# Hymba-style block with 32 routed experts: groups of three experts between the pairs, a weight ring of 22 places instead of 20, and packed small parameters

## The chip, the cores and the metric

The kernel runs on one core of a Trainium2 chip. The metric is the time of one execution on the device in microseconds, as the median of several runs. A profiled execution gives the trace that all rows below come from. In the rows PE is the matrix engine, PEld its weight loads, DVE the vector engine, ACT the scalar engine, POOL GpSimd, and SP the engine whose queue issues nearly all transfers (SPq).

## The reference, cut to what matters

One layer over 512 tokens of width 1024, all in float32. Attention comes first, the mixture of experts second.

```python
h = rms_norm(x, g_attn); proj = h @ w_in                  # 1024 -> 3072 columns
o_da = diff_attention(q1, q2, k1, k2, v, rel_bias, lam)   # 4 heads, two softmax maps each
o_sb = stick_breaking(q, k, v)                            # 8 heads
x = x + concat(rms_norm(o_da), rms_norm(o_sb)) @ w_o
h2 = rms_norm(x, g_ffn)
gsel = argmax(h2 @ wg + bg)                               # 1 of 4 expert groups
e1, e2 = top_k((h2 @ we + be)[gsel], 2)                   # 2 of its 8 experts
# for each token: the gated sum over its two experts e of
y = (silu(h2 @ w1[e]) * (h2 @ w3[e])) @ w2[e]             # 1024 -> 512 -> 1024
x = x + gate * y
```

There are 32 experts, each with three matrices of 2 MiB: 192 MiB of weights. All of them are read once in every execution, whatever the routing says.

## The kernel before, in words

**Weights as tiles of 1 MiB.** Each expert has six tiles of 128 partitions by 2048 floats: two halves of w1, two of w3, two of w2. `load_parts` issues them on SP's queue, one transfer each (L714), in the order in which the products use them. A tile lives in a place of a ring (`ring_tile`, list `slots`). The places are buffers that attention used earlier: `bt`, `qs`, `kl`, `kh` (the q8 pool), `e0`, `e1`, `n0`, `n1`, the split projection weights `w_h`, `w_l`, and the attention outputs `ma`, `mb`. The two `ma` places are used once only, because the output sums (`sums`) move into that buffer. A transfer into a place waits on SP until the last product that reads the tile there before is done, and every transfer behind it on SP waits too. One more tile, the second half of w2 of expert 1, goes to the buffers `yh` and `yl` (`load_last`, L723).

**Places of experts.** The first `FIXED` experts keep their number as their place, so their weights can be loaded before the router has run. The others are sorted by how many tokens they got, most first; `sort_experts` and `name_experts` (L1094, the int32 row `who_i`) tell SP which expert stands at a place, and SP reads that into a register (L697) before it can issue the loads. Places 0 to 19 hold up to 64 tokens (`SLOTS`), places 20 to 31 (`SMALL`) up to 32.

**Groups.** PE works through 13 groups in the order of the list `groups`: two experts of 64 token columns each, or four of 32. Either way the 128 columns of a group are one pass of the matrix engine: products whose columns lie apart run side by side. A group has 16 steps in `hidden` (w1 in two halves, w3 in two halves, four steps each; products at L1222) and 8 in `outputs` (w2; L1278). Between the steps PE gathers the tokens of the next group (L1164, L926) and adds the outputs of the one before (`combine`, L1325 and L1326). Group 7 (`PAUSE`) also holds the branch to code for experts with more tokens than slots (L1342).

**The opening.** The transposed input and the projection weights `w_raw` (pieces of 256 KiB in 4 buffers) are loaded by turns. ACT and DVE split each into a rounded high part and a rest (`x_high`, `x_low`, `high`, `low`), and PE multiplies the parts at L313. Until then `keep_clock(20)` keeps PE busy with 20 products that nothing reads (L220, two records each). ACT also squares the four tiles of `x` for the norm (`square`, L243).

**The tail.** In the last group w3's second half and w2 are loaded in smaller cuts, expert after expert for each cut, and the output is computed in five column pieces (`TAIL`, `last_product`, `last_sum`).

Of the kernel before, what the change touches and what calls it, by code (L numbers as in the profile page):

```python
# [30 lines left out]
FIXED = 4  # L31
# [63 lines left out]
def tile_block(ctx: ExitStack, tc: tile.TileContext, a: dict, out: bass.AP):  # L95
# [45 lines left out]
    oh_rel, vneg = r_tile[0:32, 0, 0:640], r_tile[0:4, 1, 0:640]  # L141
    lamv, lam_p = r_tile[:, 0, 640:896].rearrange("p (a b) -> p a b", a=4), r_tile[:, 0, 896:960]
    rb = r_tile[0:32, 1, 640:644]
# [44 lines left out]
    g_col = const.tile([P, KC], F32, name="g_col")  # L188
    nc.scalar.dma_start(g_col, a["g_attn"][0].rearrange("(p k) -> p k", k=KC))
# [3 lines left out]
    for k in range(2, KC, 2):  # L193
        load_xT(k, k + 2)
        load_w()
    for t in range(NT):
        nc.sync.dma_start(x_t[t], x_in[t])
    gqk = const.tile([P, 2], F32, name="gqk")
    gsub = const.tile([P, 1], F32, name="gsub")
    gsb = const.tile([P, 1], F32, name="gsb")  # L200
    col = lambda ap, n: bass.AP(tensor=ap.tensor, offset=ap.offset, ap=[[1, n], [1, 1]])
    for m in range(2):
        rows = slice(64 * m, 64 * m + 64)
        nc.sync.dma_start(gqk[rows, 0:1], col(a["qn_g"], 64))
        nc.sync.dma_start(gqk[rows, 1:2], col(a["kn_g"], 64))
# [9 lines left out]

    def keep_clock(n, tag="mm"):

        pb = bank(tag, (P, P))
        for _ in range(n):
            nc.tensor.matmul(pb, lhsT=ones_f, rhs=ones_f, start=True, stop=True)  # L220

    keep_clock(20)
# [29 lines left out]
    for n in range(KC // 2):  # L252
        x_high(2 * n)
        high[n]()
        x_low(2 * n)
        low[n]()
        x_high(2 * n + 1)
        x_low(2 * n + 1)

    bt = pool_q8.tile([P, 4, 512], F32, tag="bt", name="bt")  # L260
    vdram = dram.tile([4, 640], F32, name="vdram")
    def small_loads():
        nc.sync.dma_start(rb, a["rel_bias"])
        nc.sync.dma_start(oh_rel, a["rel_onehot"])
        for m in range(2):
            nc.sync.dma_start(gsb[64 * m:64 * m + 64], col(a["sb_out_g"], 64))
        nc.sync.dma_start(gsub, col(a["subln_g"], 128))
        for i, n in enumerate(("lam_q1", "lam_k1", "lam_q2", "lam_k2")):
            s = a[n]
            nc.sync.dma_start(lamv[:, i], bass.AP(tensor=s.tensor, offset=s.offset, ap=[[0, P], [1, 64]]))  # L270
# [103 lines left out]
    def h_rows(i):  # L374


        pbs = [bank("mm", (P, 2, 256)) for _ in range(2 if i == 0 else 0)]
        for k in range(0, KC // 2, 2):
            for t0, pb in zip((0, 2), pbs):
                yield from rows_bundles(h_high, h_low, split[i], t0, pb, range(k, k + 2), k == 0, False)  # L380
        for t0 in (0, 2):
            pb = pbs[t0 // 2] if pbs else bank("sc" if (i, t0) == (1, 0) else "mm", (P, 2, 256))
            yield from rows_bundles(h_high, h_low, split[i], t0, pb, range(KC // 2 if pbs else 0, KC), not pbs)
            yield t0, pb
# [261 lines left out]
    for i, (g, n, j) in enumerate(ORDER):  # L646
# [10 lines left out]
    groups = [(0, 2), (2, 2), (20, 4), (4, 2), (6, 2), (8, 2), (10, 2), (24, 4), (12, 2), (14, 2), (16, 2), (18, 2),  # L657
              (28, 4)]
# [3 lines left out]
    slots = [("q8", tag, 2) for tag in ("bt", "qs", "kl", "kh")] + [("xs", "e0", 1), ("xs", "e1", 1)]  # L662
    slots += [("q8", tag, 2) for tag in ("qs", "kl", "kh")] + [("n", "n0", 1), ("n", "n1", 1)]
    slots += [("mx", "ma", 1), ("mx", "ma", 1), ("mx", "mb", 2)]
    slots += [("w8", tag, 2) for tag in ("w_h", "w_l", "w_h", "w_l")]
    slots += [("mx", "mb", 2)]
    slots[0] = ("q8", "bt", 1)

    def ring_tile():

        pool, tag, bufs = slots[ring[0] % len(slots)]
        ring[0] += 1
        if tag == "ma":
            if ring[0] > len(slots):
                return ring_tile()
# [15 lines left out]
    def load_parts(i):  # L691
        last = i == NG - 1
        first, n_exp = groups[i]
        if first < FIXED:
            who = [first + e for e in range(n_exp)]
        else:
            who = [nc.values_load(place_id[0][0:1, first + e:first + e + 1], engines=[mybir.EngineType.SP],  # L697
                                  min_val=0, max_val=NE - 1) for e in range(n_exp)]
        t = {}
        for n, h in hidden_order(i) + [("w2", 0), ("w2", 1)]:  # L700
            src = {"w1": w1, "w3": w3, "w2": w2}[n]
# [3 lines left out]
            for c, m in zip(cuts, cuts[1:]):  # L705
                for e in range(n_exp):
                    if (i, n, h, e) == (0, "w2", 1, 1):
                        continue
                    if c == 0:
                        t[n, h, e] = ring_tile()  # L710
                    dst, part = t[n, h, e], expert(who[e], h)(src)
                    if first >= FIXED:
                        part = part.rearrange("o p f -> p (o f)")
                    nc.sync.dma_start(dst[:, c:m], part[:, c:m])  # L714
                    if m == 2048:
                        yield t
# [9 lines left out]
    loads, ahead = load_parts(0), load_parts(1)  # L726

# [29 lines left out]
    gfp = const.tile([P, 2, 4], F32, name="gfp")  # L757
# [7 lines left out]
    def router_loads():  # L765
        nc.sync.dma_start(gfp, a["g_ffn"])
        raw_r = pool_at.tile([P, KC, 64], F32, tag="qn", name="raw_r", bufs=2)
        parts = {"w_router_g": raw_r[:, 0:1, 0:32], "w_router_e": raw_r[:, 1:5]}
        for n, r in (("w_router_g", 4), ("w_router_e", 32)):
            parts[n] = parts[n].rearrange("p a b -> p (a b)").rearrange("p (h c) -> p h c", h=2)  # L770
            nc.sync.dma_start(parts[n], a[n].rearrange("p h r c -> p h (r c)"))
        for src, c0, n in ((a["b_router_g"], 0, 4), (a["b_router_e"], 4, 32)):
            nc.sync.dma_start(rbias[:, c0:c0 + n], bass.AP(tensor=src.tensor, offset=src.offset, ap=[[0, P], [1, n]]))
# [14 lines left out]
        def gains():  # L788
            for n, c0, w in (("w_router_g", 0, 4), ("w_router_e", 4, 32)):
                nc.vector.tensor_tensor(wr[:, :, c0:c0 + w], parts[n].rearrange("p h (r c) -> p (h r) c", r=4),  # L790
                                        gfp.rearrange("p h r -> p (h r)").unsqueeze(2).to_broadcast([P, KC, w]),
                                        op=ALU.mult)
# [121 lines left out]
    def match(oh, rk, ts_):  # L914
        n = ts_.stop - ts_.start
        m, w = oh.shape[2:]
# [3 lines left out]
    def gather_part(px, oh, h, ts_):  # L920

        for t in ts_:
            x2 = x_tile[0][:, t, h * 512:(h + 1) * 512].rearrange("p (r b) -> p r b", r=4)
            one = oh[:, t].rearrange("p e s -> p (e s)").bitcast(F32)
# [38 lines left out]
    for t in range(NT):  # L963
        square(t)
    token_scales()
    wv.fill(16)
# [23 lines left out]
    next(ahead)  # L990
# [21 lines left out]
    oh0 = pools["n"].tile([P, NT, 2, SLOTS], F32R, tag="oh", name="oh", bufs=1)  # L1012
    def half_match(n, t):
# [3 lines left out]
        match(oh0, rank[:, :, 0:2], slice(t, t + 2))  # L1017
# [32 lines left out]
    for _ in range(7):  # L1050
        next(ahead)
# [72 lines left out]
    def one_hot(rk, second=False):  # L1124
        n = rk.shape[-1]
        shape = [P, NT, n, P // n]
        if second:
            oh = wk("oht", shape, F32R, bufs=2)
        else:
            oh = pools["n"].tile(shape, F32R, tag="oh", name="oh", bufs=1)  # L1130
        match(oh, rk, slice(0, NT))
        return oh

    def dispatch(oh, p, px=None):
# [3 lines left out]
        ohs = [oh[:, t].rearrange("p e s -> p (e s)") for t in range(NT)]  # L1138
        n_exp, w_exp = oh.shape[2:]
        rows = [slice(w_exp * e, w_exp * e + w_exp) for e in range(n_exp)]  # L1140
        d = {"px": px, "parts": rows}

        spare = not isinstance(p, int)
# [43 lines left out]
        def finish(tag="mm"):  # L1187
# [15 lines left out]
            m = 3 * n_exp  # L1203
            g4 = pools["n"].tile([P, NT, 12], F32, tag="g4" + own, name="g4", bufs=bufs)
            c = 0 if spare else 6 * p
            for u, pb in enumerate(pbs):
                nc.scalar.copy(oht[:, 2 * u:2 * u + 2], pb[:, :, 0])
                nc.vector.tensor_copy(g4[:, 2 * u:2 * u + 2, :m], pb[:, :, 1, c:c + m])
            for e, part in enumerate(rows):
                x = 6 * (e // 2) + 2 * (e % 2)  # L1210
# [9 lines left out]
    def hidden_product(ph, d, n, h, r, e, w):  # L1220
        part = d["parts"][e]
# [3 lines left out]
    def hidden(p, t, d, between):  # L1225
# [3 lines left out]
        for n, h in hidden_order(p):  # L1229
            if n not in ph:  # L1230
                ph[n] = bank("mm")
            for r in range(4):
                for e in range(len(d["parts"])):
                    hidden_product(ph, d, n, h, r, e, t[n, h, e][:, r * HID:(r + 1) * HID])
# [53 lines left out]
    def outputs(t, ht, d, between):  # L1288
# [3 lines left out]
        for c in range(2):  # L1292
            py.append(bank("sc"))
            for j in range(4):
                for e, part in enumerate(d["parts"]):
# [33 lines left out]
    def overflow():  # L1329
# [12 lines left out]
        with tc.If(rounds > 0):  # L1342
            move(rank_s[:, :, SMALL:], SLOTS // 2)
            with tc.For_i(0, rounds, 1):
                move(rank_s, -SLOTS)
                with tc.For_i(0, NP, 1) as iv:
# [5 lines left out]
                    dd = dispatch(one_hot(rk), own)  # L1352
# [5 lines left out]
                    for n, h in hidden_order(1):  # L1358
                        for e in range(2):
                            src = (w1 if n == "w1" else w3)[bass.ds(who[e], 1), h].rearrange("o p f -> p (o f)")  # L1360
                            for r in range(0, 4, 2):
                                w = half_slot(src[:, r * HID:(r + 2) * HID])
                                for u in range(2):
                                    hidden_product(ph, dd, n, h, r + u, e, w[:, u * HID:(u + 1) * HID])
# [17 lines left out]
    def group_dispatch(i, oh=None, px=None):  # L1382
        first, n = groups[i]
        if oh is None:
            oh = one_hot((rank if first < FIXED else rank_s)[:, :, first:first + n], i == 1)
        return dispatch(oh, first // 2, px)
# [18 lines left out]
    for i in range(NG):  # L1405
# [3 lines left out]
        if not last:  # L1409
            rest = ahead if i == 0 else load_parts(i + 1)  # L1410
            for nxt in islice(rest, 1) if i == PAUSE else rest:
                pass
        during, after = [[] for _ in range(16)], [[] for _ in range(8)]
        if i == 0:
# [4 lines left out]
            during[1] = [name_experts]  # L1419
# [4 lines left out]
        else:  # L1424
            for n in range(8):
                at_ = (3 if n < 4 else 7) if last else 3 + n // 2 if i == PAUSE else 4 + n // 2 * 2
# [33 lines left out]
    def last_product(c0, c1):  # L1460
# [3 lines left out]
        for j in range(4):  # L1464
            for e, part in enumerate(d["parts"]):
# [80 lines left out]
```

## Time and profile before

| | |
|---|---|
| median of 3 runs | 752.55 us (752.36 to 755.66) |
| the profiled execution's own time | 753.97 us |
| its span in the trace | 752.3 us |
| PE / PEld busy | 726.8 us (97%) / 454.7 us (60%) |
| DVE / ACT / POOL busy | 389.1 / 302.2 / 91.7 us |
| read from HBM | 225.83 MB, mean 303 GB/s over the span |

A PE that is 97% busy is not at its peak: matmuls overlap in the pipeline and their ends are modelled, so what an engine is held by is read stage by stage. The span is what the rows show; the profiled execution took 1.67 us more than its span.

### The profile page before, as it was taken

To read this page: it belongs to the slowest core of one execution; us is meant where nothing else is said; L and a number is where in the kernel's file an instruction comes from. 1 tells how busy PE (TensorE), PEld (TensorE's weight loads), DVE (VectorE), ACT (ScalarE), POOL (GpSimd) and SP (SyncE) were. 2 spreads that over 40 slices of the span, in tenths; PEclk is the share of its full clock that TensorE was granted. 3 is DMA by queue.
4 is the path that set the end of the run, shared out by engine and by line. 5 is a ranking of instruction groups with operands and counts; after the bars stand their busy time and mean duration, and the time that the engine had idled before them with its cause. 6 is when DMAs were issued, how large, how long until landed. Compare 5 with 4: busy or idle time off the path is not lost. (4 is left out here: it accounts for less than half of the span.)

```text
span 752.3 us, 13147 instructions
## 1 busy us (share of the span) xinstructions
PE 726.8 (97%) x4812; PEld 454.7 (60%) x4812; DVE 389.1 (52%) x919; ACT 302.2 (40%) x708; POOL 91.7 (12%) x175
## 2 busy tenths in 40 slices
PE   9999999999999999999999999999779999999986
PEld 9899988887989984554435444453233444535324
DVE  4577778776665462254444554443433544444413
ACT  6665776876755340232232323221222232232100
POOL 0302100466665020000000000000000000000000
PEclk9999999999999999999999999999998999999999
DMA  8432121322573986649999999999999999999998
GB/s 314 134 127 86 54 84 57 113 58 64 166 313 112 368 362 253 240 194 381 418 419 421 421 420 422 421 421 421 416 421 419 423 419 421 422 419 420 418 409 298
DMA packets 46638, 228.86 MB, mean 304 GB/s; under 512 B 6724, under 2 KB 9412, under 8 KB 23656
## 3 DMA queue, kind: packets, MB, share of 16 engines
q1 hardware_dynamic: 46152, 227.83, 76.3%
q8 instruction: 40, 0.66, 0.3%
q14 instruction: 30, 0.25, 0.1%
q10 hardware_dynamic: 416, 0.14, 0.1%
HBM read 225.83 MB, written 2.11 MB: 303 GB/s over the span
## 5 line engine op out<-in xcount | busy, mean ns | idle before, releaser
L1156 ACT CAST part<-xs 128x256 fp32r<-128x256 f32 x176 | 63.1, 406 | 146.6 <-PE ps_mm L1164 60.1
L1157 DVE TENSOR_TENSOR part<-xs,part 128x256 fp32r<-128x256 f32 x176 | 66.6, 419 | 58.7 <-ACT part L1156 58.7
L1327 DVE TENSOR_TENSOR sums<-ps_o,sums 128x512 f32<-128x512 f32 x88 | 56.7, 686 | 71.0 <-PE ps_o L1326 71.0
L313 PE MATMUL ps_mm<-w_h,hTl 128*128 128x256 f32 x240 | 69.3, 289 | 0.1
L1222 PE MATMUL ps_mm<-qs,xt 128*64 128x512 f32 (+1 forms) x136 | 67.8, 610 | 0.0
L313 PE MATMUL ps_mm<-w_h,hTh 128*128 128x256 f32 x240 | 67.3, 281 | 0.0
L313 PE MATMUL ps_mm<-w_l,hTh 128*128 128x256 f32 x240 | 67.3, 280 | 0.0
L1222 PE MATMUL ps_mm<-mb,xt 128*64 128x512 f32 (+1 forms) x120 | 59.0, 610 | 4.1 <-PEq L1342 4.1
L1222 PE MATMUL ps_mm<-kl,xt 128*64 128x512 f32 (+1 forms) x120 | 59.3, 610 | 0.0
L1222 PE MATMUL ps_mm<-w_l,xt 128*64 128x512 f32 (+1 forms) x128 | 50.7, 602 | 0.0
L1222 PE MATMUL ps_mm<-kh,xt 128*64 128x512 f32 (+1 forms) x104 | 50.4, 600 | 0.0
L1222 PE MATMUL ps_mm<-w_h,xt 128*64 128x512 f32 (+1 forms) x120 | 46.8, 601 | 0.0
L313 PEld LDWEIGHTS ps_mm<-w_h,hTl 128*128 128x128 f32 x240 | 45.3, 189 | 0.6 <-DVE qn L438 0.3
L313 PEld LDWEIGHTS ps_mm<-w_l,hTh 128*128 128x128 f32 x240 | 45.3, 189 | 0.1
L313 PEld LDWEIGHTS ps_mm<-w_h,hTh 128*128 128x128 f32 x240 | 45.2, 188 | 0.0
L180 DVE TENSOR_TENSOR w_l<-w_raw,w_h 128x512 fp32r<-128x512 f32 x64 | 44.2, 707 | 1.0 <-ACT w_h L177 0.6
L1325 PE MATMUL ps_o<-yl,oht 128*128 128x512 f32 x96 | 43.2, 450 | 0.6 <-DVE sums L1327 0.6
L518 DVE TENSOR_TENSOR_SCAN p<-p,ones_f 128x513 f32<-128x513 f32 (+3 forms) x32 | 27.5, 858 | 30.5 <-POOL p L513 30.5
L1325 PEld LDWEIGHTS ps_o<-yl,oht 128*128 128x128 f32 x96 | 17.9, 187 | 41.8 <-issue 18.8
L1164 PEld LDWEIGHTS ps_mm<-part,oh 128*128 128x128 f32 x160 | 21.8, 191 | 33.3 <-DVE part L1157 20.3
L1251 DVE SCALAR_TENSOR_TENSOR sl<-ps_mm,rsl,sl 128x256 f32<-128x256 f32 x26 | 11.4, 479 | 58.6 <-PE ps_mm L1222 58.4
L1271 ACT ACTIVATE yh<-ps_sc,gsl 128x512 fp32r<-128x512 f32 (+2 forms) x29 | 18.5, 643 | 55.2 <-PE ps_sc L1278 55.2
(295 smaller groups left out, 1786.5 us busy)
## 6 DMA issues: line engine op xcount, KB each, us to landing
qs<-in_w SPq DMA_DIRECT2D x22, 1024.0 KB, 19.7
e<-in_w SPq DMA_DIRECT2D x22, 1024.0 KB, 19.8
kl<-in_w SPq DMA_DIRECT2D x21, 1024.0 KB, 19.7
kh<-in_w SPq DMA_DIRECT2D x21, 1024.0 KB, 19.7
n<-in_w SPq DMA_DIRECT2D x20, 1024.0 KB, 19.8
mb<-in_w SPq DMA_DIRECT2D x20, 1024.0 KB, 19.8
w_h<-in_w SPq DMA_DIRECT2D x20, 1024.0 KB, 19.8
w_l<-in_w SPq DMA_DIRECT2D x20, 1024.0 KB, 19.7
```

Of the source, the lines that this page charges most:

```text
L180: eng.tensor_tensor(part(wl, n), raw[i, n], part(wh, n).bitcast(F32), op=ALU.subtract)
L313: nc.tensor.matmul(pb[:, u], lhsT=x(t0 + u, k), rhs=y[:, k], start=first, stop=last, skip_group_check=True)
L518: nc.vector.tensor_tensor_scan(rev, rev, ones_f[:, 0:1].to_broadcast([P, n + 1]), 1.0, op0=ALU.mult, op1=ALU.mult)
L1156: nc.scalar.copy(hi, whole)
L1157: nc.vector.tensor_tensor(lo, whole, hi.bitcast(F32), op=ALU.subtract)
L1164: nc.tensor.matmul(d["rows"][:, q * 256:q * 256 + 256], lhsT=ohs[t], rhs=d[n][:, m], start=(n % 8 == 0 and m == 1), stop=(n % 8 == 7 and m ...
L1222: nc.tensor.matmul(ph[n][part], lhsT=d["xt"][h][:, r, part], rhs=w, start=(h == 0 and r == 0), stop=(h == 1 and r == 3))
L1251: nc.vector.scalar_tensor_tensor(s, ph["w3"][:, c], d["rsl"], s, op0=ALU.mult, op1=ALU.mult)
L1271: nc.scalar.activation(yh, py, AF.Copy, scale=gsl)
L1325: nc.tensor.matmul(pc, lhsT=oht[:, t], rhs=yl[:, c], start=True, stop=False)
L1327: nc.vector.tensor_tensor(sums[0][:, t, cs], pc, (xs if first else sums[0])[:, t, cs], op=ALU.add)
```

## The change

The groups become seven pairs and six threes: one expert of 64 columns and two of 32. A three is computed as four products of 32 columns (`d["cuts"]`); the two halves of the large expert read the same weight tile. `FIXED` falls from 4 to 3, so group 1 holds one expert that is known early (place 2) and two sorted ones (20 and 21): their twelve loads now follow the naming of the experts. The ring gets two more places, `n2` and `n3`, and the list `again` sets its order after the first round. Their room comes from `dynamic_dma_scratch_size=4096`, which makes the scratch for DMA descriptors smaller. The columns of group 0's outputs are added later in group 1. In the opening the small parameters come in packed arrays (`cols`, `rel`, `lam`, `w_router`, `b_router`), `keep_clock` is 15, the loads and splits stand in another order, a one-column copy (`set_up`) comes first on ACT, and the squares of `x` are split around the next weight splits.

```diff
-FIXED = 4
+FIXED = 3
...
-    for k in range(2, KC, 2):
-        load_xT(k, k + 2)
-        load_w()
-    for t in range(NT):
+    for k in range(2, KC, 2):
+        load_w()
+        load_xT(k, k + 2)
+
+    def load_x(t):
         nc.sync.dma_start(x_t[t], x_in[t])
...
-    for m in range(2):
-        rows = slice(64 * m, 64 * m + 64)
-        nc.sync.dma_start(gqk[rows, 0:1], col(a["qn_g"], 64))
-        nc.sync.dma_start(gqk[rows, 1:2], col(a["kn_g"], 64))
+    load_x(0), load_x(1)
...
+    nc.scalar.copy(const.tile([P, 1], F32, name="set_up"), ones_f[:, 0:1])
...
-    keep_clock(20)
+    keep_clock(15)
...
-    for t in range(NT):
-        square(t)
+    square(0), square(1)
+    wv.fill(8)
+    square(2), square(3)
+    wv.fill(1)
     token_scales()
-    wv.fill(16)
+    wv.fill(7)
...
-    groups = [(0, 2), (2, 2), (20, 4), (4, 2), (6, 2), (8, 2), (10, 2), (24, 4), (12, 2), (14, 2), (16, 2), (18, 2),
-              (28, 4)]
+    pair = lambda p: [(p, SLOTS), (p + 1, SLOTS)]
+    three = lambda p, q: [(p, SLOTS), (q, SLOTS // 2), (q + 1, SLOTS // 2)]
+    groups = [pair(0), three(2, 20), pair(4), three(3, 22), pair(6), three(16, 24), pair(8), three(17, 26), pair(10),
+              three(18, 28), pair(12), pair(14), three(19, 30)]
...
+    more = [("n", "n2", 1), ("work", "n3", 1)]
+    slots = early + [ma, ma, w_h, w_l, w_h, w_l, mb, mb] + more + early[:8]
+    again = early[8:] + [mb, mb] + more + [w_h] + early[0:2] + [w_l] + early[2:4] + [w_h] + early[4:6] + [w_l]
+    again += early[6:8]
...
+        step = SLOTS // 2 if len(rows) == 3 else SLOTS
+        d["cuts"] = [(e, slice(c, min(c + step, part.stop))) for e, part in enumerate(rows)
+                     for c in range(part.start, part.stop, step)]
...
-                for e in range(len(d["parts"])):
-                    hidden_product(ph, d, n, h, r, e, t[n, h, e][:, r * HID:(r + 1) * HID])
+                for e, part in d["cuts"]:
+                    hidden_product(ph, d, n, h, r, part, t[n, h, e][:, r * HID:(r + 1) * HID])
...
-            during[1] = [name_experts]
+            during[1] = [name_experts, lambda: list(ahead)]
...
-                at_ = (3 if n < 4 else 7) if last else 3 + n // 2 if i == PAUSE else 4 + n // 2 * 2
+                at_ = (3 if n < 4 else 7) if last else 8 + n if i == 1 else 3 + n // 2 if i == PAUSE else 4 + n // 2 * 2
...
-    nc = bacc.Bacc("TRN2", target_bir_lowering=False, num_devices=1)
+    nc = bacc.Bacc("TRN2", target_bir_lowering=False, num_devices=1, dynamic_dma_scratch_size=4096)
```

The order of the instructions shows three places. First, SP's queue from the last loads that need no names to the first that do. Before the change it reads (L714 and L723 are loads, TENSOR_LOAD reads an expert's number):

```order
57 L714 DMA w_l<-in_w 128x2048
58 L714 DMA mb<-in_w 128x2048
59 L723 DMA yh<-in_w 128x1024
60 L723 DMA yl<-in_w 128x1024
61 L714 DMA bt<-in_w 128x2048
62 L714 DMA qs<-in_w 128x2048
63 L714 DMA kl<-in_w 128x2048
64 L714 DMA kh<-in_w 128x2048
65 L1408 TENSOR_LOAD cint
66 L1408 ISA x2
67 L697 TENSOR_LOAD who_i
```

and of the change, where L710 and L739 are the same loads:

```order
47 L710 DMA w_l<-in_w 128x2048
48 L739 DMA yh<-in_w 128x1024
49 L739 DMA yl<-in_w 128x1024
50 L720 TENSOR_LOAD who_i
51 L720 ISA x2
52 L720 TENSOR_LOAD who_i
53 L720 ISA x2
...
55 L710 DMA mb<-in_w 128x2048
...
57 L710 DMA mb<-in_w 128x2048
...
59 L710 DMA n_3879<-in_w 128x2048
...
61 L710 DMA n_3881<-in_w 128x2048
...
63 L710 DMA bt<-in_w 128x2048
```

Two loads of `mb` and all loads from `bt` on have moved behind the reading of two names; `n_3879` and `n_3881` are the new places n2 and n3.

Second, PE at the start of group 1. Before, two products of 64 columns for each step, and the sums of group 0 (L1325, L1326) from step 4 on:

```order
1582 L1222 MATMUL ps_mm<-ma,xt 64x512 x2
1583 L1164 MATMUL ps_mm<-part,oh 128x256 x4
1584 L1222 MATMUL ps_mm<-ma,xt 64x512 x4
1585 L1164 MATMUL ps_mm<-part,oh 128x256 x4
1586 L1222 MATMUL ps_mm<-ma,xt 64x512 x2
1587 L1222 MATMUL ps_mm<-mb,xt 64x512
1588 L1222 MATMUL ps_mm<-w_h,xt 64x512
1589 L1325 MATMUL ps_o<-yl,oht 128x512
1590 L1326 MATMUL ps_o<-yh,oht 128x512
```

and of the change, where L1244 is the product and L1188 the gather:

```order
1582 L1244 MATMUL ps_mm<-ma,xt 32x512 x2
1583 L1244 MATMUL ps_mm<-mb,xt 32x512 x2
1584 L1188 MATMUL ps_mm<-part,oh 128x256 x4
...
1589 L1188 MATMUL ps_mm<-part,oh 128x256 x4
...
1592 L1244 MATMUL ps_mm<-ma,xt 32x512 x2
1593 L1244 MATMUL ps_mm<-n_3879,xt 32x512
1594 L1244 MATMUL ps_mm<-n_3881,xt 32x512
```

Each step is now four products of 32 columns: two read the large expert's tile in `ma`, one each those in the two `mb` places, and from step 4 on n2 and n3; the sums of group 0 stand further back.

Third, ACT in the opening. Before, from the first transposed input to the next weights:

```order
2 L236 ACT_TABLE_LOAD
3 L236 ACTIVATE hTh<-kh,g_col 128x512
4 L177 CAST w_h<-w_raw 128x512
...
11 L236 ACTIVATE hTh<-kh,g_col 128x512
12 L243 ACTIVATE qs,ss_150<-qs 128x1024 x4
13 L177 CAST w_h<-w_raw 128x512 x4
14 L428 ACTIVATE qn<-ps_mm 128x512 x2
```

and of the change:

```order
2 L213 ACT_TABLE_LOAD
3 L213 COPY set_up<-ones_f 128x1
4 L235 ACTIVATE hTh<-kh,cols 128x512
...
12 L235 ACTIVATE hTh<-kh,cols 128x512 x2
13 L242 ACTIVATE qs,ss_138<-qs 128x1024 x2
14 L176 CAST w_h<-w_raw 128x512 x4
15 L242 ACTIVATE qs,ss_138<-qs 128x1024 x2
16 L427 ACTIVATE qn<-ps_mm 128x512 x2
```

The table load now belongs to a copy that needs no transfer, and two of the four squares stand behind the four casts of the next weights.

## Rows read from the trace of the kernel before

**Rows 1.** Windows: length; busy us (count) of PE, PEld, DVE, ACT, POOL; clock; DMA; GB/s.

```profile
282.40:322.40 40.00, 39.42 (x234) 21.52 (x236) 10.27 (x43) 7.38 (x18) 0.00 (x0) 1.00 0.70 259
322.40:355.50 33.10, 33.10 (x162) 14.96 (x158) 16.88 (x42) 10.63 (x27) 0.00 (x0) 1.00 0.68 270
355.50:519.50 164.00, 163.99 (x890) 73.81 (x888) 77.51 (x186) 48.28 (x124) 0.00 (x0) 1.00 1.01 420
519.50:572.10 52.60, 43.74 (x266) 15.99 (x264) 19.23 (x45) 12.29 (x32) 0.00 (x0) 0.90 1.01 419
572.10:702.90 130.80, 130.78 (x639) 59.53 (x635) 61.52 (x148) 38.21 (x98) 0.00 (x0) 1.00 1.01 421
702.90:739.90 37.00, 31.73 (x237) 11.74 (x235) 8.95 (x15) 3.22 (x7) 0.00 (x0) 1.00 1.01 406
739.90:752.30 12.40, 8.37 (x122) 6.50 (x122) 5.18 (x11) 1.21 (x3) 0.00 (x0) 0.95 0.77 258
```

**Rows 2.** SP's waits (total us, times, longest); then one load's us to landing.

```profile
SPq L714 <- PE ps_mm L1222: 61.2, 22, 11.9
...
yl<-in_w SPq DMA_DIRECT2D x1, 512.0 KB, 3.2
```

**Rows 3.** Timeline of SP's queue, 268 to 336 us: start, us, load issued.

```profile
282.42 0.33 SPq L723 DMA_DIRECT2D yl<-in_w  x1
286.39 0.33 SPq L714 DMA_DIRECT2D bt<-in_w  x1
...
293.08 0.33 SPq L714 DMA_DIRECT2D kl<-in_w  x1
...
302.93 0.95 SPq L714 DMA_DIRECT2D e<-in_w  x2
311.80 0.33 SPq L714 DMA_DIRECT2D qs<-in_w  x1
...
335.01 0.33 SPq L714 DMA_DIRECT2D mb<-in_w  x1
```

**Rows 4.** DVE's row that writes the experts' names; SP's register loads of them.

```profile
284.53 0.18 DVE L1094 CAST who_i<-ps_o 1x32 int32<-1x32 f32 x1 [0.94 <-PE ps_o L1093]
...
L697 SPq TENSOR_LOAD <-who_i x28: 260/266/290, 294.8 to 665.6; - x28
```

**Rows 5.** Timeline of PE: products of 64 columns (group 0) and of 32 (group 2).

```profile
282.84 0.59 PE L1222 MATMUL ps_mm<-bt,xt 128*64 128x512 f32 x1
...
283.27 0.59 PE L1222 MATMUL ps_mm<-bt,xt 128*64 128x512 f32 x1
...
357.66 0.60 PE L1222 MATMUL ps_mm<-e,xt 128*32 128x512 f32 x2
...
358.09 0.60 PE L1222 MATMUL ps_mm<-e,xt 128*32 128x512 f32 x2
```

**Rows 6.** Timeline of PE in group 7 and in the last group.

```profile
535.78 0.72 PE L1222 MATMUL ps_mm<-mb,xt 128*32 128x512 f32 x1 [4.15 <-PEq L1342]
...
739.88 0.40 PE L1278 MATMUL ps_sc<-qs,sl 128*32 128x256 f32 x1 [0.63 <-DMA qs<-in_w]
```

**Rows 7.** Timeline of PE and of ACT in the opening.

```profile
7.00 1.75 PE L220 MATMUL ps_mm<-ones_f 128*128 128x128 f32 x14
8.51 0.36 PE L313 MATMUL ps_mm<-w_h,hTl 128*128 128x256 f32 x1
...
19.87 0.28 PE L313 MATMUL ps_mm<-w_h,hTh 128*128 128x256 f32 x1
21.25 0.39 PE L313 MATMUL ps_sc<-w_h,hTl 128*128 128x256 f32 x1 [1.10 <-ACT w_h L177]
21.98 0.39 PE L313 MATMUL ps_sc<-w_l,hTh 128*128 128x256 f32 x1 [0.34 <-DVE w_l L180]
...
4.25 1.28 ACT L236 ACT_TABLE_LOAD   x1 [4.25 <-DMA kh<-in_xT]
...
19.54 1.06 ACT L243 ACTIVATE qs<-qs 128x1024 f32<-128x1024 f32 x1 [1.78 <-DMA qs<-in_x]
```

## What I predict

> **What bounds the kernel now.** I read the windows by group first, then the waits of SP's queue, then the places on the timelines where those point. From 355.5 us on the weight stream runs without a break: 420 GB/s through groups 2 to 6, 419 and 421 after that [rows 1]. At 420 GB/s a tile of 1 MiB takes 2.50 us. PE only keeps pace: it is full while pairs run, and short in the two groups of four that come late, 43.7 us busy of 52.6 and 31.7 of 37.0 [rows 1]. So the end is set by when the last tiles land, and that by how much of the stream was lost before 355.5 us. There the reader is to see 259 GB/s in group 0 and 270 GB/s in group 1 [rows 1]. Against 420 that is 40.0 x (1 - 259/420) = 15.3 us and 33.1 x (1 - 270/420) = 11.8 us, together 27.1 us of lost stream. The waits name the cause: SP's loads waited 61.2 us for the products at L1222 to let go of a place [rows 2]. The timeline shows it, with two tiles at a time and then nothing: 286.39, 293.08, 302.93, 311.80 us, and `mb` only at 335.01 us, since the two `ma` places that group 1 frees first are not used again [rows 3].
>
> **The change, part by part.**
>
> *Loads around groups 0 and 1.* Before, 19 tiles and the two halves in `yh` and `yl` are issued without names by 282.42 us [rows 3], 20 MiB in all. Now it is 18 MiB, since one expert fewer is fixed: two tiles, 5.0 us of stream, go behind the names. The names stand in SBUF at 284.53 + 0.18 = 284.7 us; two register loads of 0.27 us and what goes with them [rows 4] put the first sorted load at about 285.8. A lone half-size load lands 3.2 us after its issue [rows 2], of which 1.25 us is its data, so a stream at rest needs about 2 us to move: 287.8 us.
>
> From then on I walk the queue. Free at once are `mb`, `mb`, n2, n3, and `bt` and `qs` from 286.4 (freed as before [rows 3]): six tiles, to 302.8 us. `kl`, `kh` (293.1) and two `e` (302.9) carry it to 312.8. The next two are freed at 311.8 and move at 313.8, a loss of 1.0; the three behind them cost about 0.7 more and last to 327.1. Then places of group 1 are needed. It starts at 322.4 and has 24 steps in 33.1 us; as an estimate its quarters of `hidden` end 5, 10, 17 and 22.5 us in, the later ones longer because the eight sums now stand there. They free 2, 2, 3 and 3 places. Waiting for the first costs 2.3 us of stream, for the third 2.1, and after that the stream is behind the places, not ahead of them. Lost in all: 287.8 - 282.4 less the 1.25 us of `yl` = 4.1, and 1.0 + 0.7 + 2.3 + 2.1, that is 10.2 us. Against 27.1 this gains 16.9; less the 5.0 us of the two tiles, **-11.9 us**. The bounds: nothing lost after 288 us (-18), or as large a share lost in group 1 as now (11.8 us, giving about -4.5). I take the middle value since every place in the walk but four is freed at a time that a row shows.
>
> The Trainium skill ("DMA: Bandwidth & Descriptors", Specifications) gives about 358 GB/s as the limit of HBM for one core; by that a tile would take 2.93 us and the gain would be 2 us larger. The trace disagrees with it, 420 GB/s for 164 us, so I go by the row.
>
> *Is PE fast enough for what comes earlier?* A group without hunger takes 164.0 / 5 = 32.8 us, and one of four experts is among those five [rows 1]. Passes of 32 columns, four side by side, start 0.43 us apart like those of 64 (358.09 - 357.66 and 283.27 - 282.84) [rows 5], so a three costs what a four does, nothing more than a pair. Group 7 has a wait of 4.15 us at the branch [rows 6], now hidden by hunger; with it and four more gathers I count 38.2 us for it. PE alone then starts the last group at 519.5 + 38.2 + 130.8 = 688.5 us, where it is 702.9 now. So the stream still ends last; PE has some 6 us in hand where it is closest (a three after two pairs, groups 9 and 12). If a group cost over 0.6 us more, that cover would be gone, and each further tenth would cost a microsecond.
>
> *The tail.* The last group has three experts. Column piece 2 waits for the last half-size cut of w2 (739.88 us now [rows 6]); behind it 1.5 MiB are still to come instead of 2, so this wait ends 0.5 MiB later in the stream: **+1.25 us**. The 12.4 us from there to the end [rows 1] I leave as they are, since they hold four products a step before and after.
>
> *The opening.* Ten records fewer of `keep_clock`: the last 14 take 8.51 - 7.00 us, 0.108 each, so real work starts 1.1 us earlier [rows 7], if its parts are ready. They should be: the table load of 1.28 us no longer stands behind the first transfer [rows 7]. The second gain is the gap between 19.87 and 21.98 us, 1.9 us over the usual step of 0.12: PE waited there for ACT's casts, and ACT for the last tile of `x`, squared at 19.54 [rows 7]. Two squares now stand behind the casts, and four tiny transfers are gone from the queue. I keep 0.5 us for new short waits: **-2.5 us**, bounds 0 and -3. PE has hardly a gap from 24 us to the first group, so what is gained at the start should reach it.
>
> *At nothing:* the packed arrays of the router and the larger count of small DVE copies (`g4`, two one-hots instead of one). DVE is idle for half of every group (16.9 us busy of 33.1 in group 1 [rows 1]); if they came on PE's path they would cost some 0.3 us a group. The smaller descriptor scratch too: SP's loads do not use GpSimd's queue.
>
> **Sum.** -11.9 + 1.25 - 2.5 = -13.15 us. The profiled execution had a span of 752.3 us and its own time of 753.97; with the change 739.2 and 740.8. The median of the runs is 752.55, 1.4 below the profiled time, so I predict **739.4 us**.
>
> **The rivals.**
>
> *The opening's gain is lost again* before group 0, because the norm of the first projection now waits for the squares that moved back. For it: eps0 and the scale on POOL hang on the last square. Against: PE reaches the first transposes a microsecond after them by my count. Then 741.9 us; chance 0.12.
>
> *The stream loses more than I walked,* because the places of a three are freed by threes and SP issues strictly in order, so that a free place waits behind a busy one. At twice the loss after 288 us, about 6 us, and more waits in group 2: 746 us; chance 0.14.
>
> *It is slower: the names or place n3 come late.* n3 lies in the pool that takes over the router's buffers, and every load behind it on SP waits with it. Up to about 291 us a delay costs nothing (group 1's first places then set the pace); each microsecond after that costs one. From about 304 us the change is slower than before; if n3 came free only with group 0's tenth step, near 309 us, it would be 757 us. Against it: what those buffers held is read before 282.4 us, when `yl` in the same pool is let through [rows 3]. Chance 0.06.
>
> *Threes cost PE more than fours,* because the two halves of the large expert read one tile at the same time, which no row shows. If they did not overlap at all, a step of 0.857 us (two passes) would become 1.28, 6 x 24 x 0.43 = 61 us in all, and the time near 790 us. Below 0.9 us it would not be seen; from about 1.03 us the change is slower. The Trainium skill ("TensorE: Matmul & The Clock Gate", Measured speedup vs the span model) has 3.07 times the speed for four packed tiles, not 4; by that, as an estimate, a step is 1.30 x 0.857 = 1.11 us and the time some 767 us. The trace disagrees for fours, with equal spacing of passes. Chance 0.03.
>
> *Better than the sum,* with the stream unbroken from 288 us: 734.5 us; chance 0.05.
>
> **How the numbers follow.** The forecast has 0.60; its own range is 736.5 to 742.5 us (the walk's estimated quarters, 2 us each way, and the opening). The range 735.5 to 746.5 holds it, the lost opening and most of the second rival, about 8 in 10. A measurement of this kernel tells some 0.5% from no change, 3.8 us, so faster means below 748.8 us: the forecast, both mild rivals and the better case, 0.91 less a little for their far ends. Chances: faster 0.90, same 0.03, slower 0.07.
>
> **What would show it.** In the changed trace: real products from about 7.4 us and no gap near 20 us; group 0 starting near 280; first sorted loads 1 to 2 us after the names; 420 GB/s reached in group 0, and more than 350 GB/s in group 1; passes of a three 0.43 us apart; short waits of PE for tiles in groups 9 and 12 and none in group 7 but the branch. I am wrong if the windows of groups 0 and 1 stay under 320 GB/s, if the stream breaks again after 355 us because PE frees places too late, or if group 0 starts no earlier.

## The result, and the profile after

| | before | with the change |
|---|---|---|
| median | 752.45 us (751.71 to 755.66, 4 runs) | 743.49 us (742.76 to 743.87, 4 runs) |
| ratio, 95% interval | | 0.9871 [0.9849, 0.9894] |
| profiled execution: own time, span | 753.97, 752.3 us | 742.76, 741.2 us |

The kernel is 1.3% faster; forecast were 739.4 us, 735.5 to 746.5. The windows of the changed kernel by group (columns as in [rows 1]):

```profile
280.90:321.00 40.10, 39.44 (x232) 21.36 (x232) 10.64 (x47) 7.38 (x18) 0.06 (x1) 1.00 0.91 361
321.00:356.60 35.60, 35.01 (x258) 13.34 (x256) 17.18 (x41) 10.64 (x27) 0.00 (x0) 1.00 0.90 354
356.60:520.80 164.20, 164.18 (x988) 72.73 (x984) 78.19 (x195) 48.33 (x124) 0.00 (x0) 1.00 1.01 421
520.80:564.30 43.50, 38.38 (x266) 14.92 (x264) 19.18 (x46) 12.20 (x32) 0.00 (x0) 0.92 1.01 418
564.30:696.70 132.40, 131.99 (x732) 58.74 (x728) 61.85 (x153) 38.21 (x98) 0.00 (x0) 1.00 1.01 421
696.70:728.70 32.00, 29.52 (x234) 11.10 (x232) 8.34 (x15) 3.22 (x7) 0.00 (x0) 1.00 1.01 402
728.70:741.20 12.50, 8.26 (x125) 6.42 (x122) 5.82 (x13) 1.21 (x3) 0.00 (x0) 0.97 0.66 219
```

Groups 0 and 1 move 361 and 354 GB/s where they moved 259 and 270 [rows 1]. Against 420 that is 40.1 x (1 - 361/420) = 5.6 us and 35.6 x (1 - 354/420) = 5.6 us of lost stream, 11.2 in place of 27.1. Groups 2 to 6 take 164.2 us as before, threes among them, so PE did not become slower. The last group takes 32.0 us up to the last cut of w2 instead of 37.0: PE waits less for tiles.

The timeline of SP's queue in those two groups (columns as in [rows 3]; L739 and L710 are the loads):

```profile
280.99 0.33 SPq L739 DMA_DIRECT2D yl<-in_w  x1
284.88 0.89 SPq L710 DMA_DIRECT2D mb<-in_w  x2
285.97 0.98 SPq L710 DMA_DIRECT2D n<-in_w  x2
...
301.56 0.91 SPq L710 DMA_DIRECT2D e<-in_w  x2
310.42 0.33 SPq L710 DMA_DIRECT2D qs<-in_w  x1
...
317.24 4.26 SPq L710 DMA_DIRECT2D n<-in_w  x2
326.37 0.91 SPq L710 DMA_DIRECT2D mb<-in_w  x2
331.86 0.91 SPq L710 DMA_DIRECT2D n<-in_w  x2
338.63 0.33 SPq L710 DMA_DIRECT2D w_h<-in_w  x1
```

The first sorted load goes out at 284.88 us, and four tiles are out by 286.95. The reader is to see the line of 326.37: the first quarter of group 1 frees two places that are used again, where before the next load stood at 335.01 us [rows 3], since a pair's first quarter frees the two `ma`. SP's waits show how little a sum of waits says. This is their first row for the products, columns as in [rows 2]:

```profile
SPq L710 <- PE ps_mm L1244: 76.1, 21, 8.5
```

It is longer than the 61.2 us of [rows 2], while the stream is nearly full: SP may wait as long as tiles that it issued earlier still keep the DMA engines busy.

The end is still set by the stream. In the chain of waits (start, us, what) the load of a last cut of w2 ends, and PE goes on behind it:

```profile
718.86 10.02 DMA qs<-in_w
728.88 0.04 issue
728.93 1.91 PE ps_sc L1300 x26
```

From 728.9 us to the end are 12.3 us, as the 12.4 behind 739.9 in [rows 1].

### The profile page after: what moved, and what is told of

It is laid out like the page before. It is cut to its first block, busy times and chain, and to the rows that moved or that the text cites. A ratio compares the mean times of both kernels' runs of the same rounds, so it can differ in the third digit from the quotient of the medians.

```text
span 741.2 us, 13696 instructions
## 1 busy us (share of the span) xinstructions
PE 721.2 (97%) x5090; PEld 448.8 (61%) x5090; DVE 391.5 (53%) x936; ACT 302.3 (41%) x709; POOL 92.1 (12%) x175
## 4 chain that ended last, share of the span: by engine, by line
PE 70%; DMA 22%; DVE 3%; ACT 2%; issue 1%; POOL 1%; SPq 0%; DVEq 0%; POOLq 0%; ACTq 0%
PE ps_mm L1244 18%; PE ps_mm L312 14%; PE ps_sc L1300 9%; DMA mb<-in_w 4%; DMA kh<-in_w 4%; PE ps_o L1347 3%; PE ps_mm L1188 3%; DMA n<-in_w 3%; DMA bt<-in_w 3%; DMA kl<-in_w 3%; DMA w_l<-in_w 3%; PE ps_tr L936 2%; PE ps_o L1348 2%; PE ps_sc L1188 2%; PE ps_mm L321 2%; PE ps_o L528 2%
## 5 line engine op out<-in xcount | busy, mean ns | idle before, releaser
L1244 PE MATMUL ps_mm<-n,xt 128*32 128x512 f32 (+1 forms) x232 | 69.4, 616 | 4.7 <-PEq L1364 4.4
L1244 PE MATMUL ps_mm<-kl,xt 128*32 128x512 f32 (+1 forms) x144 | 59.1, 601 | 0.0
L1244 PE MATMUL ps_mm<-kh,xt 128*32 128x512 f32 (+1 forms) x120 | 55.2, 602 | 0.0
L1244 PE MATMUL ps_mm<-w_h,xt 128*32 128x512 f32 (+1 forms) x144 | 50.9, 599 | 0.0
L1244 PE MATMUL ps_mm<-qs,xt 128*32 128x512 f32 (+1 forms) x112 | 50.3, 600 | 0.0
L1347 PE MATMUL ps_o<-yl,oht 128*128 128x512 f32 x96 | 43.4, 452 | 0.6 <-DVE sums L1349 0.6
L1244 PE MATMUL ps_mm<-w_l,xt 128*32 128x512 f32 (+1 forms) x120 | 42.7, 599 | 0.0
L1188 PEld LDWEIGHTS ps_mm<-part,oh 128*128 128x128 f32 x160 | 21.3, 188 | 32.1 <-DVE part L1181 16.5
L1287 ACT COPY sl<-ps_mm 128x256 f32<-128x256 f32 x26 | 10.1, 387 | 75.0 <-PE ps_mm L1283 75.0
L176 ACT CAST w_h<-w_raw 128x512 fp32r<-128x512 f32 x64 | 38.0, 619 | 4.9 <-DMA w_raw<-in_w_in 4.6
```

Of the source, the lines that this page charges most:

```text
L176: nc.scalar.copy(part(wh, n), raw[i, n])
L1188: nc.tensor.matmul(d["rows"][:, q * 256:q * 256 + 256], lhsT=ohs[t], rhs=d[n][:, m], start=(n % 8 == 0 and m == 1), stop=(n % 8 == 7 and m ...
L1244: nc.tensor.matmul(ph[n][part], lhsT=d["xt"][h][:, r, part], rhs=w, start=(h == 0 and r == 0), stop=(h == 1 and r == 3))
L1347: nc.tensor.matmul(pc, lhsT=oht[:, t], rhs=yl[:, c], start=True, stop=False)
```

## The experiments

Each ratio is to the kernel before, on the same chip, with its 95% interval. Chips differ (its median was 752.5 to 754.2), so the ratios are compared.

### Are the places and the groups worth something apart?

**22 places without threes, and neither.** The groups, the number of fixed experts, the order of places and the steps of group 0's sums are those of before, in the changed kernel:

```diff
-    slots = early + [ma, ma, w_h, w_l, w_h, w_l, mb, mb] + more + early[:8]
...
+    slots = early + [ma, ma, mb, w_h, w_l, w_h, w_l, mb] + more
+    again = early + [mb, w_h, w_l, w_h, w_l, mb] + more
...
-    groups = [pair(0), three(2, 20), pair(4), three(3, 22), pair(6), three(16, 24), pair(8), three(17, 26), pair(10),
...
+    groups = [pair(0), pair(2), four(20), pair(4), pair(6), pair(8), pair(10), four(24), pair(12), pair(14), pair(16),
```

and `more = []` in the second kernel.

> The changed kernel with the old groups (pairs and fours, four fixed experts, sums of group 0 from step 4) and the old order of places, n2 and n3 added behind it: 22 places alone. The earlier kernel with old groups had the two mb places where group 1 lets go of them last, at 345 us; here they come free near 335 us as before. Theory (each place more is one tile of 2.5 us that need not wait, whatever the groups): 5.0 us under the next kernel, 745 to 747 us. Rival (two places bring nothing without threes): 750 to 752 us.

> The same without n2 and n3: the order of SP's loads is that of the kernel before, and only the opening and the packed parameters are left of the change. Theory: group 0 starts 1.2 to 1.4 us earlier and the whole stream with it, 751 to 751.5 us. Rival (the opening is not carried to the end): 752.5 us.

Measured: 750.35 us, 0.9939 [0.9926, 0.9952] with 22 places, and 753.52 us, 0.9995 [0.9982, 1.0008] with 20. Two places bring 0.0056 x 752.5 = 4.2 us without any three (3.2 by the two medians); the theory had 5.0. The opening by itself cannot be told from nothing. Windows of groups 0 and 1, with 22 places and then with 20:

```profile
282.30:323.50 41.20, 40.63 (x232) 22.26 (x234) 10.04 (x43) 7.38 (x18) 0.00 (x0) 0.96 0.76 300
323.50:356.50 33.00, 33.00 (x163) 15.10 (x159) 16.92 (x45) 10.62 (x27) 0.00 (x0) 1.00 0.68 268
```

```profile
281.80:321.70 39.90, 39.31 (x232) 21.48 (x234) 10.19 (x43) 7.38 (x18) 0.06 (x1) 1.00 0.69 258
321.70:354.70 33.00, 33.00 (x163) 15.02 (x159) 16.90 (x44) 10.64 (x27) 0.00 (x0) 1.00 0.68 269
```

The places help group 0 (300 against 258 GB/s) and do nothing for group 1 (268 against 269), where the pair's first quarter still lets go of nothing that can be loaded. That part came with the threes.

**Threes without the two places:**

```diff
-    more = [("n", "n2", 1), ("work", "n3", 1)]
+    more = []
```

> The changed kernel with n2 and n3 left out, so 20 places again; groups of three and the opening stay. Theory (the two parts need each other: threes free places three at a time, and only with two more places does the stream not stop between them): the walk of the queue, made again with these places, loses 10 us more stream than with 22, so nearly the whole gain goes: 750 to 752 us, and group 1's window falls from 354 to about 300 GB/s. Rival (each part has its own share of the gain): 746 to 748 us.

Measured: 753.06 us, 1.0017 [1.0001, 1.0033]. The four ratios, from 752.5 us:

| | 20 places | 22 places |
|---|---|---|
| pairs and fours | 0.9995, -0.4 us | 0.9939, -4.6 us |
| threes | 1.0017, +1.3 us | 0.9871, -9.7 us |

In the orders of places that were run the parts need each other: threes bring +1.7 us with 20 places and -5.1 with 22, each known to about 2 us either way. The row of the threes holds more than the groups: three fixed experts, the late sums and an order of places of its own go with them, and none of these was run by itself. The time is 1 us above the theory's range, but the stream came out as expected, 293 GB/s in group 1 for about 300:

```profile
280.40:320.50 40.10, 39.39 (x232) 21.36 (x232) 10.64 (x48) 7.38 (x18) 0.10 (x1) 1.00 0.80 311
320.50:356.00 35.50, 34.90 (x258) 13.36 (x256) 17.06 (x41) 10.64 (x27) 0.00 (x0) 1.00 0.74 293
```

That is 10.4 + 10.7 = 21.1 us of lost stream, 9.9 more than with 22 places. SP's timeline of the kernel with threes and 20 places says why:

```profile
325.92 0.92 SPq L710 DMA_DIRECT2D mb<-in_w  x2
338.17 0.33 SPq L710 DMA_DIRECT2D w_h<-in_w  x1
338.71 0.33 SPq L710 DMA_DIRECT2D bt<-in_w  x1
```

The gap of 12 us stands where n2 and n3 were loaded at 331.86 us. A part of it belongs to the order of places: `w_h` comes free with the third quarter, and `bt`, which by my reading of the code held tiles of the second, is queued behind it. A better order for 20 places was not tried, so the 11 us that n2 and n3 bring with threes is their worth in this order only.

**What an order of places costs.** Two first kernels with the old groups, in which the eight places behind the early ones kept the changed kernel's order (`ma, ma, w_h, w_l, w_h, w_l, mb, mb`) and the sums of group 0 its late steps; 22 places, then 20.

> The changed kernel with the old groups (pairs and fours, four experts with fixed places), the 22 places and the opening kept. Theory (the parts need each other): group 2, the four, wants 24 tiles at once from places that a pair frees, so the walk loses 10 us more: 750 to 752 us, and PE waits for tiles in the last group and in group 7 again. Rival (own shares): 746 to 748 us.

> The changed kernel with the old groups and 20 places: what is left is the opening and the packed parameters. Both theories: 750.5 to 752 us, the opening's 1.4 us under the kernel before at most; group 0 starts at 280.9 us as with the change.

Measured: 758.53 us, 1.0068 [1.0049, 1.0088], and 763.08 us, 1.0136 [1.0113, 1.016]: both expectations fell, by the same 10 us that separate them from the two kernels above. SP's timeline and the window of group 1 with 22 places:

```profile
316.93 4.84 SPq L711 DMA_DIRECT2D n<-in_w  x2
345.54 0.90 SPq L711 DMA_DIRECT2D mb<-in_w  x2
```

```profile
321.20:356.90 35.70, 35.10 (x163) 14.14 (x158) 17.58 (x44) 10.63 (x27) 0.00 (x0) 1.00 0.38 148
```

With pairs `mb, mb` is what the last quarter reads. SP's queue stood from 321.8 to 345.5 us, and group 1 got 148 GB/s. The late sums lengthen group 1 too (35.7 us against 33.0), so 10 us is for both. The larger share is the queue's stop: late sums move the last quarter's release by only 1.3 us (24.3 us into the group, 23.0 in the kernel with early sums and 22 places), while the stop lasts 23.7 us instead of 12.1.

### What holds the end: the stream or PE?

**No branch in group 7:**

```diff
-                during[7] += [overflow, lambda: list(rest), partial(begin, i + 1)]
+                during[7] += [lambda: list(rest), partial(begin, i + 1)]
```

> The changed kernel without the branch in group 7 and the code for experts with more tokens than slots, which this routing does not need. PE lost 4.4 us at the branch and some 3 us at half clock behind it. Theory (the stream ends last, PE is close behind it): PE gets 7 us in hand and the time falls by 0 to 1.5 us, to 742 to 743.5 us. Rival (PE has become the bound): the time falls by 5 to 7 us, to 736.5 to 738.5 us.

Measured: 743.42 us, 0.9879 [0.9855, 0.9902], the same. Group 7 and, later, group 9 in the windows:

```profile
521.60:558.40 36.80, 36.03 (x266) 14.52 (x264) 19.02 (x46) 12.10 (x32) 0.00 (x0) 1.00 1.01 420
591.60:635.00 43.40, 39.33 (x258) 15.95 (x256) 16.04 (x39) 10.18 (x26) 0.00 (x0) 0.92 1.01 420
```

PE gets 6.7 us back in group 7 (36.8 against 43.5) and loses more than that in group 9 (43.4 us, where the changed kernel takes 34.6), waiting for tiles. The stream ends last.

**More work for PE:** `during[14].append(lambda: keep_clock(18, "o"))` in group 3.

> The changed kernel with 18 products of ones that nothing reads put into group 3 (two records of 0.108 us each, 3.9 us of PE). Theory (PE waits for tiles 0.5 to 1 us in all from group 2 to the last group, so that much is in hand and no more): 746 to 747 us. Rival (PE has 6 us in hand, as the prediction counted): 743 to 744 us, no change.

Measured: 744.21 us, 0.9872 [0.9847, 0.9897]: no change, so my theory of 0.5 to 1 us in hand fell: 3.9 us more of PE do not show, as the 6 us of the prediction have it. The profiled execution gives a size. By chance it had also started group 0 late and lost clock in it, so PE came to the last group 705.75 - 696.71 = 9.0 us later than with the change alone, and the span was only 4.4 us longer: 4.6 us were in hand. I had taken the listed waits (about 1 us) for all the hunger. It is not: the last group's `hidden` takes 22.1 us with the change and 19.2 us here, where tiles were always there, and the waits view shows 0.4 us of that.

### The opening

**`keep_clock(20)`** instead of 15:

> The changed kernel with keep_clock(20) instead of 15: the first real product comes 1.1 us later, at 8.2 us. Theory (the gap near 21 us is set by the weight pieces that land at 20.9 us, not by PE's start): the gap shrinks by as much, group 0 starts within 0.3 us of 280.9, and the time stays within 0.5 us of 743.5. Rival (what the opening gained came from the shorter keep_clock): group 0 starts at 282.0 and the time is 744.6.

Measured: 743.99 us, 0.9877 [0.9853, 0.9902]; group 0 at 281.43 us. The rival's 282.0 and the theory's 281.2 are both 0.6 us or less away, and nine profiles with the changed kernel's opening have group 0 start anywhere from 280.46 to 282.70 us. The records of the products give a direction. The same product of the first projection (the 111th record) starts at 23.64 us before, 20.43 with the change and 21.67 here, and 40 records later the change and this kernel are 0.24 us apart (28.52 and 28.76). In between, PE waits with the change:

```profile
7.15 0.37 PE L312 MATMUL ps_mm<-w_h,hTl 128*128 128x256 f32 x1
...
21.76 0.39 PE L312 MATMUL ps_sc<-w_h,hTl 128*128 128x256 f32 x1 [0.69 <-ACT w_h L176]
22.49 0.39 PE L312 MATMUL ps_sc<-w_l,hTh 128*128 128x256 f32 x1 [0.34 <-DVE w_l L179]
...
21.09 0.62 ACT L176 CAST w_h<-w_raw 128x512 fp32r<-128x512 f32 x1 [1.69 <-DMA w_raw<-in_w_in]
```

ACT's cast, and PE behind it, wait for a piece of the weights. By this pair, whoever starts earlier waits longer there. It is one pair: in the nine profiles the first real product starts at 6.33 to 7.61 us, and the later of the two records stands anywhere from 28.16 to 30.33.

**Squares behind two casts:** the first two squares of `x` after `wv.fill(4)` instead of before `wv.fill(8)`.

> The changed kernel with the first two squares of x behind the first two of the next four weight casts, so that the buffers of these pieces come free 2.3 us earlier. Theory (the gap of 1.5 us near 21 us is the first two squares again, one buffer round later): the casts stand at about 13 us, the next pieces are issued at about 14.3 instead of 16.6 us, the gap goes, group 0 starts near 279.6 and the time is 742.0 to 742.5. Rival (the pieces are late for want of bandwidth, or the wait moves to the norm): no change, 743.5.

Measured: 742.95 us, 0.986 [0.9836, 0.9884], and the gap unchanged (1.67 us from start to start, in two pieces): the theory fell. The casts stood at 16.03 us instead of 13, since they waited 1.90 us for pieces that had not landed, so the squares do not hold the pieces up.

**`x` later:**

```diff
-        if n in (1, 2):
-            load_x(n + 1)
...
-    wv.fill(8)
+    wv.fill(4)
+    load_x(2)
+    wv.fill(2)
+    load_x(3)
+    wv.fill(2)
```

> The changed kernel with the third and fourth tile of x loaded behind four more weight pieces instead of between them. Theory (up to 21 us the DMA engines are full, and the pieces for which PE waits at 20.4 to 22.5 us stand behind 1 MiB of x): the two gaps of 1.7 us go, group 0 starts at 279.3 to 279.9 us and the time is 742 to 742.5. Rival (the wait moves to the norm or to the next pieces): no change of group 0's start beyond 0.4 us, 743 to 744 us.

Measured: 746.78 us, 0.9895 [0.988, 0.991] (by the ratio 744.5 us on the chip of the result). The gaps near 21 us are gone, so the pieces did stand behind `x`; but the norm now waits for the last square, which is the rival. PE's row and two windows:

```profile
29.20 0.58 PE L310 MATMUL ps_mm<-w_h,hTl 128*128 128x256 f32 x1 [2.96 <-DVE qn L435]
```

```profile
25.90:29.20 3.30, 0.34 (x3) 0.05 (x1) 2.21 (x5) 2.02 (x5) 3.21 (x3) 0.80 0.00 0
29.20:34.00 4.80, 4.80 (x22) 4.80 (x23) 2.30 (x5) 0.98 (x2) 1.04 (x2) 0.50 0.25 78
```

Behind 3.3 us of nearly idle PE the granted clock is 0.50, that is 1.2 GHz, for 4.8 us and more, and group 0 started only at 284.77 us.

**And gathers later:** as the last, and in group 1 the gathers four steps later (`n // 2 * 2 - 4 + late`).

> As the last, and in group 1 the gathers for group 2 stand four steps later, so that PE lets go of the places of the first three quarters 1.3 us earlier. Theory (in group 1 the stream waits for PE's places, mb at 326.4 and n at 331.9 us): group 1's window gains 1.3 us of stream, 1 to 1.5 us under the last kernel, 740.5 to 741.5 us. Rival (the loss only moves to the last quarter): the same time as the last kernel.

Measured: 744.89 us, 0.9886 [0.9867, 0.9904] (by the ratio 743.9 us). The intervals overlap, so this is not settled. The profiles, one of each kernel, speak for the theory: both start group 1 within 0.1 us (325.01 and 324.93), `mb` and n2 go out 1.5 and 2.0 us earlier (328.69 and 333.74 against 330.22 and 335.70), and the span is 1.6 us shorter. From 280 to 325 us both streams moved the same (14.5 to 14.6 MB); from 325 to 360 us this one moves 374 GB/s where the last kernel has 354, which is 1.7 us of stream. The gathers alone, with the change's opening, were not run.

### Must a three be cut into four?

```diff
-        step = SLOTS // 2 if len(rows) == 3 else SLOTS
+        step = SLOTS
```

> The changed kernel with a three computed as three products, of 64, 32 and 32 columns, instead of four of 32. Theory (the pass is 0.43 us and products whose columns lie apart share it, whatever their widths): no change, 743.5 within 1 us, passes of a three 0.43 us apart. Rival (only products of one width run side by side): a step of a three needs two passes instead of one and costs 0.4 to 0.9 us more, 24 steps in six groups, 60 us or more: above 790 us.

Measured: 886.94 us, 1.1757 [1.1729, 1.1785]. The largest effect of the study, and in the direction of the rival, far past it. PE's timeline with the cuts (the changed kernel, a step in group 3) and without:

```profile
389.85 0.62 PE L1244 MATMUL ps_mm<-kh,xt 128*32 128x512 f32 x2
389.87 0.62 PE L1244 MATMUL ps_mm<-w_h,xt 128*32 128x512 f32 x1
389.87 0.62 PE L1244 MATMUL ps_mm<-e,xt 128*32 128x512 f32 x1
390.31 0.60 PE L1244 MATMUL ps_mm<-kh,xt 128*32 128x512 f32 x2
```

```profile
420.48 1.07 PE L1244 MATMUL ps_mm<-kh,xt 128*64 128x512 f32 x2
421.48 0.62 PE L1244 MATMUL ps_mm<-w_h,xt 128*32 128x512 f32 x1
421.48 0.62 PE L1244 MATMUL ps_mm<-e,xt 128*32 128x512 f32 x1
421.93 0.59 PE L1244 MATMUL ps_mm<-w_h,xt 128*32 128x512 f32 x1
421.94 0.59 PE L1244 MATMUL ps_mm<-e,xt 128*32 128x512 f32 x1
422.46 1.07 PE L1244 MATMUL ps_mm<-kh,xt 128*64 128x512 f32 x2
```

Cut, the four products start within 0.02 us and the next pass 0.44 us later. Uncut, the two products of 32 run side by side, but only after the one of 64, and the step takes 422.46 - 420.48 = 1.98 us, not 0.86. Each width's two passes are 0.86 us; the 0.26 us left over are, by this count, 0.13 us for each of the two changes of width. 6 groups x 24 steps x 1.12 us = 161 us of PE, of which 143 us show. The Trainium skill ("TensorEngine Tiling (Array Packing)", Key Properties) says that a change of tiling mode drains the engine; the trace agrees: the products of the two widths do not overlap.

## Why the prediction was right

The range and the direction held; the point was 4.1 us too low.

- **Places, names, stream.** The walk had the first sorted load at 285.8 us without the earlier opening; it went out at 284.88. It had group 1's quarters 5, 10, 17 and 22.5 us in; the loads that they release stand 5.3, 10.8 and 17.6 us in, and the last one 24.2. It lost 10.2 us where the windows show 11.2, so the gain is 27.1 - 11.2 - 5.0 = 10.9 us, not 11.9. The kernels with parts undone show that the mechanism was this one.
- **The opening** was over-sized: -2.5 us, measured -1.4 between the two profiles. Even that may be in part chance: the nine profiles with this opening start group 0 at a median of 281.73 us, 0.6 us before the one profile of the kernel before (282.36), and the kernel with nothing but the opening and the packed arrays is at -0.4 us, within 1 us either way. The step that failed is adding two gains, the shorter `keep_clock` and the gap near 20 us, each by its own row. They stand in series: by the 97th record PE is 2.5 us ahead (18.75 against 21.25 us), and then it loses 1.5 us over the usual steps, waiting for weight pieces, where the kernel before loses 0.6. So the gap near 20 us, whose absence was to be a sign, is still there.
- **The tail**, +1.25 us: the stream's wait moved from 739.88 to 728.93 us, 10.95 us, against 10.9 + 1.4 us gained before it, so 1.35 as the remainder; neither it nor the 5.0 us of the two tiles has a run of its own.
- **PE fast enough.** Right in its result, with 4.6 us in hand for 6. Group 7 was counted at 38.2 us, with the wait at the branch in it, and took 43.5. Of the 5.3 us, 2.5 are lost at nearly half clock behind the branch (below), which the count did not have. Most of the rest is the group's own work: without the branch it takes 36.8 us, where the count leaves 38.2 - 4.15 = 34.05. Of groups 9 and 12 only 12 stands behind two pairs.
- **Threes cost no more than a pair.** Groups of three take 33.1 us, the pairs beside them 33.2. The Trainium skill ("TensorE: Matmul & The Clock Gate", Measured speedup vs the span model) has 3.07 times for four tiles packed by rows, from which the prediction's estimate of a step was 1.11 us; the four tiles here are packed by columns, and 0.86 was measured. The rival that gave threes two passes a step was the right danger, and it was bigger than priced: a mixed step costs 1.98 us, not 1.28. What keeps it away is the cut into equal widths.
- **The median.** Of the 4.1 us, 1.0 is the stream's and, by the two profiles, 1.1 the opening's. The other 2.1 are no mechanism: the profiled execution of before was 1.4 us over its median and I kept that distance, and the one of after was 0.7 us under it.

## What to carry to other kernels

Where a queue issues loads in order into a ring, walk it place by place: when each is freed, which load stands next, and whether it can go at all. More places and a better rhythm of release can together be worth far more than the sum of each alone, as in the orders that were run here; and a wrong order of places, with the late sums, cost about as much as the whole change gained. Before a gain at the start of a program is added up, look for the next wait behind it; and give products that are to share the array one width.

## What the runs showed of the hardware

**A stop costs PE twice.** Around the branch of the changed kernel, two windows:

```profile
532.90:537.40 4.50, 0.06 (x4) 0.03 (x1) 0.17 (x1) 0.12 (x1) 0.00 (x0) 0.80 1.01 417
537.40:543.00 5.60, 5.60 (x24) 1.92 (x24) 2.04 (x5) 2.26 (x7) 0.00 (x0) 0.55 1.02 415
```

PE idles 4.5 us, and the next 5.6 us run at a granted clock of 0.55, most of it 1.2 of 2.4 GHz, 2.5 us more of lost work; without the branch group 7 was 6.7 us shorter. The 3.3 us of the kernel with `x` later did the same. The two gaps near 21 us, 1.7 us together, did not.

**Clock lost without such a stop.** In four profiles of the twelve experiments (more PE, no cuts, 22 places with the old groups, gathers later) group 0's `hidden` took 30.3 to 31.8 us from its first product to its last instead of 28.8 to 28.9. In the first of them the clock falls to 0.50 between two groups of gathers, with no gap between products over 1.24 us near it:

```profile
294.00:298.00 4.00, 3.36 (x20) 2.44 (x20) 1.19 (x4) 0.33 (x1) 0.00 (x0) 0.78 1.02 430
298.00:302.00 4.00, 4.00 (x14) 2.17 (x14) 0.00 (x0) 0.00 (x0) 0.00 (x0) 0.50 1.01 418
```

The changed kernel has the same gap of 1.24 us at 293.94 us and kept its clock. What decides it is open.
